# Value products of the prompt's attention in groups of three key blocks, with a compressed branch of fixed width 128, in a decoder step on one core

## The chip, the cores and the metric

The kernel runs on one core of a Trainium2 chip. The metric is the device time of one execution in microseconds, the median of the runs. The engines are named as in the profile: PE is TensorE's matmul, PEld its weight load, DVE is VectorE, ACT is ScalarE, POOL is GpSimd, SP is SyncE.

## What is computed

One layer of a decoder works on 1024 prompt tokens and on 64 sample tokens (8 sequences of 8), with the same weights. Half of its heads are gated linear attention; the other half are sparse attention with 8 query heads on 2 key heads. After them come an output projection, norms and an MLP. The change lies in the sparse attention, which for each query sums three branches, each a softmax of its own, times a gate:

```python
s_c = einsum('bqhgd,bchd->bqhgc', qb, kc) - sl * d_c      # compressed keys: one per 16 tokens
p_c = masked_softmax(s_c, d_c >= 0)
o_c = einsum('bqhgc,bchd->bqhgd', p_c, vc32)
...                                                       # o_s: selected blocks, o_w: window of 512
o_n = gts[..., 0:1] * o_c + gts[..., 1:2] * o_s + gts[..., 2:3] * o_w
```

In the prompt all earlier blocks are selected, so the selected branch there is plain causal attention. The sample tokens attend to a cache of 2048 tokens in pages.

## The kernel before

The instructions are traced by Python code in program order; a planner then sets, at build time, the order on each engine: among the instructions that it holds to be ready, the one that comes first in program order goes first. Each engine runs its own list in that order, and an instruction that isn't ready holds back all that stand behind it on its engine.

**The prompt's attention** (`attention`, lines 1146 to 1250) works in four parts of two query tiles of 128 tokens, in the order `for i in (1, 0, 2, 3)` (line 689). `tt` is the number of the query tile (0 to 7) and `kvh` that of the key head. For each pair of them the loop of lines 1231 to 1247 runs three branches: the compressed one, whose width is `wc = 8 * tt + 8` keys (line 1222), the window (128 to 640 keys) and the selected one (128 to 1024 keys).

- `branch` (line 1163) makes the weights of one branch. For each of four query heads, two matmuls (L1177, L1178) put the scores into a bank of tag `dn`, DVE adds the mask and finds the largest (L1180), ACT takes the exponential (L1184), and POOL scales by gate and sum (L1190). The four results are tiles of tag `Sc`, `Sw` or `Ss`; `SW` and `SS` (line 26) say how many buffers of `Sw` and `Ss` each part has.
- `values` (line 1194) goes over the branch in blocks of 128 keys. For each block PE transposes the four heads' weights into a bank of tag `g`, of which there are three (L1200), ACT copies the bank to a tile `pw`, of which there are three (L1202), and two matmuls add the product with the block's values to the bank `av` (L1205). The first of the two fills partitions 0 to 63 of `av` and the second 64 to 127: each uses 64 of the array's columns. Both are in fp32 and stand as two records each in the trace, so a block has four records at L1205 and four at L1200. The compressed branch is one block, of 8 to 64 rows.

The value products of a branch are traced after the next branch's `branch` (`later`, line 1245), so that scores and softmax of one lie beside the products of the other.

**Fillers.** Other work is traced in between (lines 686 to 696), in proportion to the attention's work as `total` (line 37) counts it: in the first three parts the sample's selection and attention (`sample_select`, `sample_attention`), in the last part the output projection of parts 0 and 1 (`wout`, L259 to L261). The sample's scores (`scores`, line 1343) begin with a matmul that puts mask and distance into the bank (L1345), with 9 or 64 rows of tables in `cstr`, and go on with two matmuls of 64 columns each (L1347). Its own value products (`weigh`, L1384 to L1390) are made in halves of 64 columns, too.

**Order of the work.** The attention begins while the projections before it run out, near 626 us of the trace, and ends near 1062 us, where the output projection of the last two parts and the MLP follow.

Of the kernel before, what the change touches and what calls it, by code (L numbers as in the profile page):

```python
# [9 lines left out]
F32 = mybir.dt.float32  # L10
F32R = mybir.dt.float32r
# [10 lines left out]
BIG = 1e30  # L22
SLOPES = [2.0 ** -(h + 1) for h in range(8)]
CHUNKS = [(0, 384, 384), (384, 384, 384), (768, 256, 320)]
TILES = [(128 * i, 128) for i in range(8)] + [(NP, NS)]
SW, SS = (8, 8, 8, 7), (8, 8, 8, 5)
H2 = [(0, 256), (256, 128), (384, 128), (512, 256), (768, 320)]
# [9 lines left out]
def total(part):  # L37
    return 2 * sum(8 * t + 8 + 128 * min(t + 1, 5) + 128 * (t + 1) for t in (range(6) if part < 3 else (6, 7)))

def shape_constants():
    c = {}
    p = np.arange(128)
    c["ident"] = np.eye(128, dtype=np.float32)
    r = np.arange(-896, 128)
    d = p[:, None] - r[None, :]
    big = {}
    big["m_sel"] = np.where(d >= 0, -d, -BIG).astype(np.float32)
    d = p[:, None] - np.arange(128)[None, :] + 512  # L50
    big["m_old"] = np.where(d <= 512, -d, -BIG).astype(np.float32)
    r = np.arange(-56, 8)
    d = p[:, None] - 16 * r[None, :] - 31
    c["m_cmp"] = np.where(d >= 0, -d, -BIG).astype(np.float32)
    c["row_valid"] = (p >= 31).astype(np.float32)[:, None]
    qs = np.zeros((128, 4), np.float32)
    for j in range(4):
        qs[:64, j] = 0.125 / SLOPES[2 * j]
        qs[64:, j] = 0.125 / SLOPES[2 * j + 1]
    c["qscale"] = qs  # L60
    j, i = p[:, None], p[None, :]
    tri = ((j // 16 == i // 16) & (j <= i)).astype(np.float32) / 16
    bi = (j < 16 * np.arange(10)[None, :]).astype(np.float32) / 16
    c["tri"] = np.concatenate([tri, bi], 1)
    m, q = np.arange(64)[None, :] // 16, p[:, None] // 16
    c["odd"] = (q == 2 * m).astype(np.float32)
    m8 = np.zeros((128, 64), np.float32)
    j, i = np.arange(64)[:, None], np.arange(64)[None, :]
    m8[:64] = (j // 8 == i // 8) & (j <= i)
    c["mask8"] = m8  # L70
    c["tri8"] = m8 / 16
    bm = np.zeros((128, 8), np.float32)
    bm[:] = (np.arange(128) % 64)[:, None] // 8 == np.arange(8)[None, :]
    c["bmask"] = bm
    c["ones"] = np.ones((128, 128), np.float32)
    c["pick"] = (np.isin(p[:, None] - np.arange(24)[None, :], (32, 96))).astype(np.float32)
    return c, big
# [144 lines left out]
class Prog:  # L222
# [845 lines left out]
    def compressed_keys(self, st, st2):  # L1068
        nc, a = self.nc, self.a
        kc = self.pool(st, "kc")  # L1070
        self.KC = self.t(kc, [128, 2, 2, 64], F32R, "KC")
        self.VC = self.t(kc, [64, 2, 64], F32, "VC")
        nc.vector.memset(self.KC.bitcast(F32), 0.0)
# [5 lines left out]
        for kind in range(2):  # L1079
# [7 lines left out]
            ps = self.bank("dn")[:M, :256]  # L1087
# [58 lines left out]
    def attention(self, st):  # L1146
        nc, a = self.nc, self.a
        pool = self.pool(st, "att")
# [10 lines left out]
        nc.vector.tensor_scalar(first, first, self.C("row_valid"), None, op0=OP.mult)  # L1159
        m_sel, m_old, m_cmp = big[:, :1024], big[:, 1024:], self.C("m_cmp")  # L1160


        def branch(tt, kvh, QS, br, vb, k0, pieces):
            K = self.KC[:, kvh] if vb is None else self.KK[vb][:, kvh, :, k0:]
            width = pieces[-1][0] + pieces[-1][1]
            wide = 256 * (tt // 2 + 1)
            shape, tag, bufs = {None: (64, "Sc", 4), 1: (min(640, wide), "Sw", SW[tt // 2]),
                                0: (wide, "Ss", SS[tt // 2])}[vb]
# [24 lines left out]

        def values(av, kvh, S, width, vb, k0, first, last):
            for c in range(0, width, 128):
                cw = min(128, width - c)
                V = self.VC[:cw, kvh] if vb is None else self.VV[:, vb, (k0 + c) // 128, 64 * kvh:64 * kvh + 64]
                pt = self.bank("g")[:cw]
                for g in range(4):
                    nc.tensor.transpose(pt[:, 128 * g:128 * g + 128], S[g][:, c:c + cw], self.C("ident"))  # L1200
                pw = t([128, 512], "pw", 3)[:cw]
                nc.scalar.copy(pw, pt)  # L1202

                for j in range(2):
                    nc.tensor.matmul(av[64 * j:64 * j + 64], V, pw.rearrange("p (a j q) -> p j a q", a=2, j=2)[:, j],  # L1205
                                     start=first and c == 0, stop=last and c + 128 >= width)

        def part_attention(i):
            later = None
            for tt in range(2 * i, 2 * i + 2):  # L1210
# [5 lines left out]
                for j in range(2):  # L1216
# [4 lines left out]
                kend = 128 * (tt + 1)  # L1221
                wc = 8 * tt + 8

                branches = [
                    (0, None, 0, [(0, wc, m_cmp[:, 56 - 8 * tt:64])]),
                    (2, 1, w0, ([(0, 128, m_old)] if tt > 3 else []) +
# [4 lines left out]
                for kvh in range(2):  # L1231
                    box = []
                    for n, (br, vb, k0, pieces) in enumerate(branches):
                        S, width = branch(tt, kvh, QS, br, vb, k0, pieces)

                        def after(box=box, n=n, kvh=kvh, S=S, width=width, vb=vb, k0=k0, catn=self.catn, c0=c0):
                            if n == 0:
                                box.append(self.bank("av")[:, :256].rearrange("p (a q) -> p a q", a=2))
                            values(box[0], kvh, S, width, vb, k0, n == 0, n == 2)
                            if n == 2:  # L1240
                                nc.scalar.copy(catn[:, 2 * kvh:2 * kvh + 2, c0:c0 + 128], box[0])
                            return width


                        if later:
                            yield later()
                        later = after
# [6 lines left out]
    def sample_select(self, keep, pool):  # L1254
# [29 lines left out]
        for pr in range(4):  # L1284
            ps = self.bank("mm")[:, :128]
            self.scores(ps, pr, lambda b2: kc[:, 2 * pr + b2], self.R2("l_t")[:9], self.R2("r_cmp")[:9])
            mx, sm = t([128, 1], "mx", 4), t([128, 1], "sm", 4)
# [72 lines left out]
    def sample_attention(self, pool):  # L1360
# [31 lines left out]

        lt = self.R2("l_t")[:9]
        zero = C("zero")
        for pr in range(4):
            mx, sm = t([128, 3], "mxs", 2), t([128, 2], "sms", 2)
            new = self.R2("oh_tok")[:64, 128 * pr:128 * pr + 128], self.R2("r_new")[:64]
            vc = t([128, 2, 128], "vc")
# [9 lines left out]
            ps = self.bank("mm")  # L1408
            self.scores(ps, pr, lambda b2: wk[:, b2], lt, self.R2("r_win")[:9])
            self.add_max(W[:, :512], ps, zero.to_broadcast([128, 512]), None, mx[:, 0:1])  # L1410
# [17 lines left out]
            for q in range(4):  # L1428
                ps = self.bank("mm")
                self.scores(ps, pr, lambda b2: pages[q][b2][:, :, :128], lt,  # L1430
                            self.R2("r_slc")[:9, None, :].to_broadcast([9, 8, 64]))
                self.add_max(S[:, 512 * q:512 * q + 512].rearrange("p (b i) -> p b i", i=64),
# [336 lines left out]
```

## Time and profile before

| | us |
|---|---|
| median of 3 runs | 1901.11 (1900.35 to 1906.42) |
| the profiled execution, its own time | 1902.94 |
| its span, from first to last instruction | 1901.3 |
| PE busy in the span | 1798.7 (95%) |
| DVE / ACT / POOL busy | 1130.0 / 938.8 / 333.9 |
| mean granted clock of TensorE, as a share of full speed | 0.97 |

The profiled execution is 1.8 us over the median of the runs. Matmul records overlap and their ends are modelled, so PE's busy share doesn't tell how well it is used; the starts of successive records do, and the rows below are read that way: a row's start, subtracted from that of the next row, is what the row took of PE's time.

### The profile page before, as it was taken

Reading aid. Unit: us, or ns where it says so; the run is one execution under the profiler, and the core shown is the slowest. Engines: PE = TensorE matmul, PEld = TensorE weight load, DVE = VectorE, ACT = ScalarE, POOL = GpSimd, SP = SyncE. Lnnn points to the kernel's source line nnn. Section 1 sums busy time; section 2 is a strip of 40 time slices with the busy share of each in tenths; the row PEclk is TensorE's granted clock in tenths of the full one; section 3 lists DMA queues with packets and bytes.
Section 4 is the critical chain, followed back from the end, with each engine's and each line's share of the span. In section 5 each row is a group of like instructions: output and inputs, shape, how many; then the busy total and the mean of one; then the engine's idle time right before and its main releaser. Section 6 shows DMA issues by size and latency. Waiting matters only on the chain.

```text
span 1901.3 us, 33235 instructions
## 1 busy us (share of the span) xinstructions
PE 1798.7 (95%) x12006; PEld 1617.3 (85%) x12006; DVE 1130.0 (59%) x2551; ACT 938.8 (49%) x1913; POOL 333.9 (18%) x502
## 2 busy tenths in 40 slices
PE   4999989999999999999999899999999999999997
PEld 3888889999989755655586799899999999999996
DVE  7867785374434664454636656856566668655555
ACT  4423355353233666555746556543443354654453
POOL 4433210012401446334322100000000001000000
PEclk9999999999999988989999899999999999999998
DMA  7666641113455423213122356321222155564442
GB/s 248 227 228 231 221 138 59 31 47 136 158 192 161 150 75 113 86 56 112 60 70 85 107 194 202 103 78 56 59 75 87 59 157 176 194 205 150 149 151 88
DMA packets 117194, 245.97 MB, mean 129 GB/s; under 512 B 14475, under 2 KB 72637, under 8 KB 116230
## 3 DMA queue, kind: packets, MB, share of 16 engines
q1 hardware_dynamic: 101254, 196.98, 32.6%
q0 software_dynamic: 13328, 43.99, 6.7%
q10 hardware_dynamic: 2448, 2.88, 0.4%
q8 instruction: 94, 1.54, 0.3%
q14 instruction: 70, 0.57, 0.1%
HBM read 215.88 MB, written 32.05 MB: 130 GB/s over the span
## 4 chain that ended last, share of the span: by engine, by line
PE 77%; issue 7%; DVE 7%; DMA 5%; ACT 2%; POOL 1%; SPq 1%; POOLq 0%; DVEq 0%; ACTq 0%
PE mm L259 10%; PE mm L260 10%; PE mm L261 10%; PE dn L259 5%; PE dn L260 5%; PE dn L261 5%; PE g L1200 4%; PE av L1205 4%; PE g L260 3%; PE g L259 3%; PE g L261 3%; PE dn L1177 2%; DMA wr<-w_ada 2%; PE dn L1178 2%; PE mm L1347 1%
## 5 line engine op out<-in xcount | busy, mean ns | idle before, releaser
L254 DVE TENSOR_TENSOR wl<-wr,wh 128x1024 fp32r<-128x1024 f32 x174 | 213.2, 1225 | 215.4 <-ACT wh L253 214.0
L253 ACT CAST wh<-wr 128x1024 fp32r<-128x1024 f32 (+1 forms) x176 | 183.4, 1043 | 241.5 <-PE mm L260 107.8
L259 PE MATMUL dn<-fh,wh 128*128 128x384 f32 (+1 forms) x616 | 204.3, 332 | 5.2 <-DVE fo L1610 2.9
L260 PE MATMUL dn<-fl,wh 128*128 128x384 f32 (+1 forms) x616 | 203.4, 330 | 0.0
L261 PE MATMUL dn<-fh,wl 128*128 128x384 f32 (+1 forms) x616 | 202.9, 330 | 0.0
L599 POOL TENSOR_TENSOR rs_r<-rs_m,mhalf 128x2 f32<-128x2 f32 (+2 forms) x12 | 13.1, 1090 | 710.4 <-DVE rs_m L598 710.4
L259 PE MATMUL mm<-hT,wh 128*128 128x384 f32 (+1 forms) x384 | 128.7, 335 | 6.0 <-ACT st L801 3.4
L260 PE MATMUL mm<-hT,wh 128*128 128x384 f32 (+1 forms) x384 | 128.1, 334 | 0.0
L261 PE MATMUL mm<-hT,wl 128*128 128x384 f32 (+1 forms) x384 | 127.4, 333 | 0.4 <-DVE wl L254 0.4
L259 PEld LDWEIGHTS dn<-fh,wh 128*128 128x128 f32 x616 | 115.7, 188 | 8.1 <-DVE fo L1610 4.2
L260 PEld LDWEIGHTS dn<-fl,wh 128*128 128x128 f32 x616 | 115.8, 188 | 0.3 <-DVE fl L254 0.3
L261 PEld LDWEIGHTS dn<-fh,wl 128*128 128x128 f32 x616 | 115.7, 188 | 0.1
L1202 ACT COPY pw<-g 128x512 f32<-128x512 f32 (+3 forms) x148 | 81.6, 587 | 63.9 <-PE g L1200 63.2
L1610 DVE TENSOR_TENSOR fo<-fo,dn 128x384 f32<-128x384 f32 (+1 forms) x134 | 72.3, 540 | 55.6 <-PE dn L261 55.4
L259 PE MATMUL mm<-w1h,wh 128*128 128x256 f32 x256 | 77.7, 304 | 21.1 <-ACT wh L253 16.2
L1205 PE MATMUL av<-pw,VV 128*64 128x256 f32 x528 | 86.7, 415 | 1.0 <-ACT pw L1202 1.0
L1177 PE MATMUL dn<-KK,QS 128*128 128x512 f32 (+3 forms) x192 | 76.9, 404 | 7.0 <-DVE mx L1180 6.6
L259 PE MATMUL mm<-cth,wh 128*128 128x256 f32 (+1 forms) x256 | 75.9, 298 | 4.5 <-ACT cth L253 4.5
L259 PEld LDWEIGHTS mm<-hT,wh 128*128 128x128 f32 x384 | 73.4, 191 | 7.9 <-ACT st L801 3.6
L261 PE MATMUL mm<-x2h,wl 128*128 128x320 f32 x256 | 79.3, 310 | 0.7 <-DVE wl L254 0.7
L259 PE MATMUL mm<-x2h,wh 128*128 128x320 f32 x256 | 79.2, 309 | 0.0
L260 PE MATMUL mm<-x2l,wh 128*128 128x320 f32 x256 | 79.1, 309 | 0.0
(623 smaller groups left out, 5418.4 us busy)
## 6 DMA issues: line engine op xcount, KB each, us to landing
wr<-w_up SPq DMA_DIRECT2D x72, 512.0 KB, 3.6
wr<-w_down SPq DMA_DIRECT2D x72, 512.0 KB, 3.6
wr<-w_ada SPq DMA_DIRECT2D x48, 512.0 KB, 4.4
wr<-w_f SPq DMA_DIRECT2D x24, 512.0 KB, 3.6
wr<-cw SPq DMA_DIRECT2D x16, 512.0 KB, 4.3
wr<-w_out SPq DMA_DIRECT2D x16, 512.0 KB, 3.5
raw<-cc SPq DMA_DIRECT2D x62, 128.0 KB, 4.8
raw<-cc POOLq DMA_DIRECT2D x61, 128.0 KB, 5.2
```

The lines of the kernel that those rows point to most:

```text
L253: return (self.nc.scalar.copy(h, src), (lo or self.nc.vector).tensor_tensor(l, src, h.bitcast(F32), op=OP.subtract))
L254: (lo or self.nc.vector).tensor_tensor(l, src, h.bitcast(F32), op=OP.subtract))
L259: mm(out, ah, bh, start=start, stop=False)
L260: mm(out, ah, bl, start=False, stop=False)
L261: mm(out, al, bh, start=False, stop=stop)
L1177: nc.tensor.matmul(ps, q, K[:, 0, c:c + cw], start=True, stop=False)
L1178: nc.tensor.matmul(ps, q, K[:, 1, c:c + cw], start=False, stop=True)
L1200: nc.tensor.transpose(pt[:, 128 * g:128 * g + 128], S[g][:, c:c + cw], self.C("ident"))
L1202: nc.scalar.copy(pw, pt)
L1205: nc.tensor.matmul(av[64 * j:64 * j + 64], V, pw.rearrange("p (a j q) -> p j a q", a=2, j=2)[:, j], start=first and c == 0, stop=last and ...
L1347: mm(ps[64 * b2:64 * b2 + 64], self.Q[:, 2 * pr + b2], keys(b2), start=False, stop=True)
L1610: nc.vector.tensor_tensor(o, o, ps, op=OP.add)
```

## The change

In the prompt's attention the value products of a block aren't issued behind the block's copy any more. The block is put on a list, and when three blocks are on it, or the last block of the last branch has come, the products of all are issued one after another. The list runs on over the border from one branch to the next, within one query tile and key head. The products of the first blocks of a group get a dependence on the copy of the last one. There are six `pw` buffers instead of three, and in the last part five and four buffers of `Sw` and `Ss` instead of seven and five.

The compressed branch always works on 128 keys, the later ones masked; its mask, wider now, moves from the table `cst` to `cst3`. `KC`, `VC` and `Sc` grow to 128 keys. The mask matmuls of the sample's scores read all 128 rows of their tables instead of 9 or 64; the added rows are zero on one side.

```diff
+GROUP, PW = 3, 6
-SW, SS = (8, 8, 8, 7), (8, 8, 8, 5)
+SW, SS = (8, 8, 8, 5), (8, 8, 8, 4)
...
-    return 2 * sum(8 * t + 8 + 128 * min(t + 1, 5) + 128 * (t + 1) for t in (range(6) if part < 3 else (6, 7)))
+    return 2 * sum(128 + 128 * min(t + 1, 5) + 128 * (t + 1) for t in (range(6) if part < 3 else (6, 7)))
...
-    r = np.arange(-56, 8)
+    r = np.arange(-56, 128)
     d = p[:, None] - 16 * r[None, :] - 31
-    c["m_cmp"] = np.where(d >= 0, -d, -BIG).astype(np.float32)
+    big["m_cmp"] = np.where(d >= 0, -d, -BIG).astype(np.float32)
...
-        self.KC = self.t(kc, [128, 2, 2, 64], F32R, "KC")
-        self.VC = self.t(kc, [64, 2, 64], F32, "VC")
+        self.KC = self.t(kc, [128, 2, 2, 128], F32R, "KC")
+        self.VC = self.t(kc, [128, 2, 64], F32, "VC")
...
-        def values(av, kvh, S, width, vb, k0, first, last):
+        def values(box, kvh, S, width, vb, k0, last):
             for c in range(0, width, 128):
-                cw = min(128, width - c)
-                V = self.VC[:cw, kvh] if vb is None else self.VV[:, vb, (k0 + c) // 128, 64 * kvh:64 * kvh + 64]
-                pt = self.bank("g")[:cw]
+                V = self.VC[:, kvh] if vb is None else self.VV[:, vb, (k0 + c) // 128, 64 * kvh:64 * kvh + 64]
+                pt = self.bank("g")
                 for g in range(4):
-                    nc.tensor.transpose(pt[:, 128 * g:128 * g + 128], S[g][:, c:c + cw], self.C("ident"))
-                pw = t([128, 512], "pw", 3)[:cw]
-                nc.scalar.copy(pw, pt)
-
-                for j in range(2):
-                    nc.tensor.matmul(av[64 * j:64 * j + 64], V, pw.rearrange("p (a j q) -> p j a q", a=2, j=2)[:, j],
-                                     start=first and c == 0, stop=last and c + 128 >= width)
+                    nc.tensor.transpose(pt[:, 128 * g:128 * g + 128], S[g][:, c:c + 128], self.C("ident"))
+                pw = t([128, 512], "pw", PW)
+                box["group"].append((V, pw, nc.scalar.copy(pw, pt)))
+                end = last and c + 128 >= width
+                if len(box["group"]) < GROUP and not end:
+                    continue
+                for n, (V, pw, ins) in enumerate(box["group"]):
+                    for j in range(2):
+                        m = nc.tensor.matmul(box["av"][64 * j:64 * j + 64], V,
+                                             pw.rearrange("p (a j q) -> p j a q", a=2, j=2)[:, j],
+                                             start=box["first"], stop=end and n == len(box["group"]) - 1)
+                        if n < len(box["group"]) - 1:
+                            tc.add_manual_dep(m.ins, box["group"][-1][2].ins.name, mybir.DependencyInfo(
+                                mybir.DependencyClass.Sync, mybir.DependencyReason.DATA), reason="group")
+                    box["first"] = False
+                box["group"] = []
...
-                    (0, None, 0, [(0, wc, m_cmp[:, 56 - 8 * tt:64])]),
+                    (0, None, 0, [(0, 128, m_cmp[:, 56 - 8 * tt:184 - 8 * tt])]),
...
-        lt = self.R2("l_t")[:9]
+        lt = self.R2("l_t")
...
-            new = self.R2("oh_tok")[:64, 128 * pr:128 * pr + 128], self.R2("r_new")[:64]
+            new = self.R2("oh_tok")[:, 128 * pr:128 * pr + 128], self.R2("r_new")
...
-            self.scores(ps, pr, lambda b2: wk[:, b2], lt, self.R2("r_win")[:9])
+            self.scores(ps, pr, lambda b2: wk[:, b2], lt, self.R2("r_win"))
```

## Rows read from the trace of the kernel before

**Rows 1.** The page: busy us of the engines, their share of the span, instructions.

```profile
PE 1798.7 (95%) x12006; PEld 1617.3 (85%) x12006; DVE 1130.0 (59%) x2551; ACT 938.8 (49%) x1913; POOL 333.9 (18%) x502
```

**Rows 2.** Stretches: length, busy us of PE, PEld, DVE, ACT, POOL; clock, DMA share, GB/s.

```profile
626.00:1062.00 436.00, 415.31 (x2787) 277.30 (x2785) 228.07 (x894) 272.14 (x711) 163.62 (x258) 0.95 0.28 85
...
960.00:1000.00 40.00, 40.00 (x306) 35.12 (x305) 15.48 (x34) 19.05 (x40) 3.44 (x4) 1.00 0.22 67
```

**Rows 3.** Timeline of PE: start, us, instruction, records; a run, and blocks alternating.

```profile
959.64 1.15 PE L1200 MATMUL g<-cst,Ss 128*128 128x128 f32 x9
960.54 0.49 PE L1177 MATMUL dn<-KK,QS 128*128 128x512 f32 x1
...
1055.74 0.66 PE L1200 MATMUL g<-cst,Ss 128*128 128x128 f32 x4
1056.33 0.65 PE L1205 MATMUL av<-pw,VV 128*64 128x256 f32 x4
1056.92 0.66 PE L1200 MATMUL g<-cst,Ss 128*128 128x128 f32 x4
...
1059.84 1.52 PE L1205 MATMUL av<-pw,VV 128*64 128x256 f32 x12
```

**Rows 4.** Timeline of PE: the first row of value products.

```profile
643.17 0.65 PE L1205 MATMUL av<-pw,VC 24*64 24x256 f32 x4
```

**Rows 5.** Timeline of PE: a mask matmul of the sample, and prompt scores before value products.

```profile
701.03 0.31 PE L1200 MATMUL g<-cst,Ss 128*128 128x128 f32 x1
701.27 0.50 PE L1345 MATMUL mm<-cstr 9*128 9x512 f32 x1
701.70 1.08 PE L1347 MATMUL mm<-wr,Q 128*64 128x512 f32 x4
...
1007.46 0.40 PE L1178 MATMUL dn<-KK,QS 128*128 128x512 f32 x1
1007.79 0.65 PE L1205 MATMUL av<-pw,VV 128*64 128x256 f32 x2
```

**Rows 6.** Timeline of PE: scores with 8 and with 128 keys.

```profile
705.43 0.25 PE L1178 MATMUL dn<-KC,QS 128*128 128x8 f32 x1
705.54 0.25 PE L1177 MATMUL dn<-KC,QS 128*128 128x8 f32 x1
...
708.88 0.28 PE L1177 MATMUL dn<-KK,QS 128*128 128x128 f32 x1
708.99 0.27 PE L1178 MATMUL dn<-KK,QS 128*128 128x128 f32 x1
```

**Rows 7.** Lines 1180, 1184, 1190, 1202: count, ns min/median/max, first and last start, forms.

```profile
L1180 DVE CUSTOM_DVE_ANT_0 Sc<-dn,cst x64: 158/192/227, 629.3 to 1015.4; 128x24 f32<-128x24 f32 x8, 128x32 f32<-128x32 f32 x8, 128x8 f32<-128x8 f32 x8, 128x16 f32<-128x16 f32 x8
L1180 DVE CUSTOM_DVE_ANT_0 Sw<-dn,big x64: 277/292/692, 635.0 to 1028.1; 128x128 f32<-128x128 f32 x40, 128x384 f32<-128x384 f32 x8, 128x512 f32<-128x512 f32 x8, 128x256 f32<-128x256 f32 x8
L1184 ACT ACTIVATE Sc<-Sc,mx x64: 284/324/367, 629.5 to 1015.7; 128x24 f32<-128x24 f32 x8, 128x32 f32<-128x32 f32 x8, 128x8 f32<-128x8 f32 x8, 128x16 f32<-128x16 f32 x8
L1184 ACT ACTIVATE Sw<-Sw,mx x64: 384/779/860, 636.0 to 1032.1; 128x640 f32<-128x640 f32 x32, 128x384 f32<-128x384 f32 x8, 128x512 f32<-128x512 f32 x8, 128x128 f32<-128x128 f32 x8
L1190 POOL TENSOR_SCALAR Sc<-Sc,sm,gates x62: 336/367/1352, 639.2 to 1017.8; 128x24 f32<-128x24 f32 x8, 128x32 f32<-128x32 f32 x8, 128x8 f32<-128x8 f32 x8, 128x16 f32<-128x16 f32 x8
L1190 POOL TENSOR_SCALAR Sw<-Sw,sm,gates x62: 437/864/1800, 641.2 to 1036.6; 128x640 f32<-128x640 f32 x30, 128x384 f32<-128x384 f32 x8, 128x512 f32<-128x512 f32 x8, 128x128 f32<-128x128 f32 x8
L1202 ACT COPY pw<-g x148: 558/586/621, 641.6 to 1060.0; 128x512 f32<-128x512 f32 x132, 24x512 f32<-24x512 f32 x2, 32x512 f32<-32x512 f32 x2, 8x512 f32<-8x512 f32 x2
```

**Rows 8.** Who waited for line 1202's copies: us in total, times.

```profile
  PEld av L1205: 6.6, 17
  PE av L1205: 1.0, 3
```

**Rows 9.** Timeline of PE, query tile 6: transposes that free `Sw`, scores into it.

```profile
922.51 0.66 PE L1200 MATMUL g<-cst,Sw 128*128 128x128 f32 x4
...
929.21 0.49 PE L1177 MATMUL dn<-KK,QS 128*128 128x512 f32 x1
```

More of the change, by code (lines that the diff above doesn't have):

```diff
@@ L1146, in attention @@
     def attention(self, st):
-        nc, a = self.nc, self.a
+        nc, tc, a = self.nc, self.tc, self.a
         pool = self.pool(st, "att")
@@ L1159, in attention @@
         nc.vector.tensor_scalar(first, first, self.C("row_valid"), None, op0=OP.mult)
-        m_sel, m_old, m_cmp = big[:, :1024], big[:, 1024:], self.C("m_cmp")
+        m_sel, m_old, m_cmp = big[:, :1024], big[:, 1024:1152], big[:, 1152:]
         def branch(tt, kvh, QS, br, vb, k0, pieces):
@@ L1166, in branch @@
             wide = 256 * (tt // 2 + 1)
-            shape, tag, bufs = {None: (64, "Sc", 4), 1: (min(640, wide), "Sw", SW[tt // 2]),
+            shape, tag, bufs = {None: (128, "Sc", 4), 1: (min(640, wide), "Sw", SW[tt // 2]),
                                 0: (wide, "Ss", SS[tt // 2])}[vb]
@@ L1221, in part_attention @@
                 kend = 128 * (tt + 1)
-                wc = 8 * tt + 8
                 branches = [
-                    (0, None, 0, [(0, wc, m_cmp[:, 56 - 8 * tt:64])]),
+                    (0, None, 0, [(0, 128, m_cmp[:, 56 - 8 * tt:184 - 8 * tt])]),
                     (2, 1, w0, ([(0, 128, m_old)] if tt > 3 else []) +
@@ L1231, in part_attention @@
                 for kvh in range(2):
-                    box = []
+                    box = {"group": [], "first": True}
                     for n, (br, vb, k0, pieces) in enumerate(branches):
@@ L1237, in after @@
                             if n == 0:
-                                box.append(self.bank("av")[:, :256].rearrange("p (a q) -> p a q", a=2))
-                            values(box[0], kvh, S, width, vb, k0, n == 0, n == 2)
+                                box["av"] = self.bank("av")[:, :256].rearrange("p (a q) -> p a q", a=2)
+                            values(box, kvh, S, width, vb, k0, n == 2)
                             if n == 2:
-                                nc.scalar.copy(catn[:, 2 * kvh:2 * kvh + 2, c0:c0 + 128], box[0])
+                                nc.scalar.copy(catn[:, 2 * kvh:2 * kvh + 2, c0:c0 + 128], box["av"])
                             return width
@@ L1285, in sample_select @@
             ps = self.bank("mm")[:, :128]
-            self.scores(ps, pr, lambda b2: kc[:, 2 * pr + b2], self.R2("l_t")[:9], self.R2("r_cmp")[:9])
+            self.scores(ps, pr, lambda b2: kc[:, 2 * pr + b2], self.R2("l_t"), self.R2("r_cmp"))
             mx, sm = t([128, 1], "mx", 4), t([128, 1], "sm", 4)
@@ L1430, in sample_attention @@
                 self.scores(ps, pr, lambda b2: pages[q][b2][:, :, :128], lt,
-                            self.R2("r_slc")[:9, None, :].to_broadcast([9, 8, 64]))
+                            self.R2("r_slc")[:, None, :].to_broadcast([128, 8, 64]))
                 self.add_max(S[:, 512 * q:512 * q + 512].rearrange("p (b i) -> p b i", i=64),
```

## The prediction, put down before the change was run

> **What bounds the kernel now.** I read four views, in this order. The page puts PE at 95% of the span, far over DVE and ACT [rows 1], so what shortens PE's list shortens the kernel, if PE is really at work in the stretch that changes. The table by stretches shows that for the attention, 626 to 1062 us: PE 415 of 436 us, DVE 228, ACT 272, POOL 164 [rows 2]. So PE is the bound there, with some 21 us of visible idle time. The granted clock tells a second thing: its mean is 0.95, against 1.00 at 960 to 1000 us, where the output projection fills PE [rows 2]. As the levels are 2.4 and 1.2 GHz, 0.95 means a tenth of the stretch, some 44 us, at the lower one, which costs at most half of that, 22 us.
>
> The third view, PE's timeline, shows what those 415 us hide. The starts tell what a row takes. Nine transposes in a row take 960.54 - 959.64 = 0.90 us, or 0.10 each. Where single blocks alternate, the four transposes of one take 1056.33 - 1055.74 = 0.59 us, against 0.40 to 0.44 for the same four in a row, and the products of one 1056.92 - 1056.33 = 0.59 us. Three blocks' products in a row are a row of 1.52 us against 0.65 for one, so a further block costs (1.52 - 0.65) / 2 = 0.43 [rows 3]. Each way between full-width matmuls and products of 64 columns thus loses about 0.15 us (0.59 - 0.44, and 0.59 - 0.43): **0.30 us for a visit to the products and back**, however many blocks it holds. No engine is waited for in these rows; the array itself changes over.
>
> The fourth view, the count. There are 148 blocks (the copies in the row of line 1202 [rows 7]). From the first row of products [rows 4] to the last [rows 3] the timeline has some 125 runs of them, nearly all of four records, one block. 125 visits at 0.30 are 38 us of the stretch.
>
> **The change, part by part.**
>
> *Fewer visits.* A query tile and key head has 1 + min(tt + 1, 5) + tt + 1 blocks: 3, 5, 7, 9, 11, 12, 13, 14 for tt = 0 to 7. In threes, with the rest, these are 1, 2, 3, 3, 4, 4, 5, 5 groups, over two heads 54. All products of a group become ready with one copy, so they come out in one run unless something that stands before them in program order becomes ready in between. I take 60 runs, ends 54 and 90. Of the 125 runs now, about a tenth stand right beside other products in halves (the sample's), where a visit has less to lose. So (125 - 60) x 0.30 x 0.93 = 18 us less; ends (125 - 90) x 0.30 x 0.93 = 10 and (125 - 54) x 0.30 = 21.
>
> *The sample's mask matmul.* With 9 rows it takes 701.70 - 701.27 = 0.43 us before the products in halves follow, and 0.24 lie between the transpose before it and itself, against 0.10 between transposes. A matmul over 128 rows of as many columns is followed by products in halves after 1007.79 - 1007.46 = 0.33 us [rows 5]. So full rows save some 0.10 behind it and 0.10 ahead. There are 32; 20 have 512 columns, 12 fewer, for which I count the 0.10 ahead alone: 20 x 0.20 + 12 x 0.10 = 5.2 us, less the ten or so that come right behind products in halves and have nothing to save ahead: 4 us. Ends 2 and 6.
>
> *128 keys in the compressed branch.* On PE, 128 score matmuls grow from 8 to 64 columns to 128. From one to the next it is 0.11 us with 8 columns and 0.11 with 128 [rows 6], as another weight load lies between, so I count 0. The Trainium skill says otherwise (TensorE: Matmul & The Clock Gate, Back-to-back issue gap): some 60 cycles up to 64 columns, 134 at 128. By it each would take 74 cycles more, an estimate of 31 ns at 2.4 GHz, 4 us in all, and the sum below would be 16 us. The trace doesn't agree with it for these pairs. Elsewhere the branch pays: DVE's mask step takes 0.19 us (median) for `Sc` and 0.28 to 0.29 for 128 keys (the window's least and median), ACT's exponential 0.32 against 0.38 (the window's least, 128 keys) [rows 7]; 64 of each, 6.4 and 3.8 us. POOL's step I bound by ACT's, the same number of elements: under 4 us. All three engines have 160 us or more free in the stretch [rows 2], and these scores are made a branch ahead of their transposes. 0; without that cover the chain of four heads would show, 0.5 us in each of 16 rounds: 8 us.
>
> *The new wait.* A group's first product stands on PE's list behind its third copy. What stands behind it there is everything else of PE: the next blocks' transposes, scores, fillers, and through them DVE's mask steps and ACT's copies. Today products wait 6.6 + 1.0 us for copies, 20 times [rows 8], since each is listed with other PE work before it. A copy takes 0.59 us [rows 7], a block's transposes 0.44, so the third copy of a group ends about 3 x 0.59 - 3 x 0.44 + 0.44 = 0.9 us after the third block's transposes, if ACT does nothing else. There are three `g` banks, so the next block's transposes (0.44) can go in that gap as soon as the first copy has freed one, beside scores and fillers. I take 2 us more of waiting in all; ends -5 (54 waits in place of 148) and 8 (half of the groups, 0.3 each).
>
> *Buffers and fillers.* In the last part `Sw` falls to five, `Ss` to four. Five mean that of the second key head's four `Sw` tiles one is free at once. Before, its last scores stood at 929.21 anyway, 6.7 us after the last transposes of the first head's tiles began at 922.51 [rows 9]; the heads two and three can start no later than that last one does. 0, upper end 4. The new `total` moves a few fillers by one step: 0. A wider `cst3` is one load long before its use: 0.
>
> *The sum.* -18 - 4 + 0 + 2 + 0 = **-20 us**, all of it on PE's list in the attention, against the profiled execution's 1902.9 (its span and 1.6 us around it): 1883. That execution is 1.8 us over the median of the runs, so on the median it is 1881, and I say **1880**. What is late next is still PE: the stretch would be 416 us with DVE at 234 and ACT at 276.
>
> **The rivals.**
>
> *The clock rises, too (about 1869).* If the time at 1.2 GHz comes from changing over, 65 visits fewer take part of it away. For: 960 to 1000 us, with hardly a change-over, has 1.00 [rows 2]. Half of the 22 us back is -11: 1880 - 11.
>
> *The groups don't hold (about 1892).* If the planner puts other work between the products of a group, or lists them so late that PE idles, the change does little of what it says: a third of the visits' gain, 6, and the 4 of the mask matmuls, less 2: 8 to 10 us, 1892. Against: of the runs now nearly none is shorter than a block, though a block is four records that could be parted as well.
>
> *The clock falls (about 1900, no change).* Twelve transposes now come in a row, then a gap for the copy. If the array counts as idle during them, the lower level takes 88 us instead of 44 and gives back 22. Against: nine transposes in a row stand just before a stretch at 1.00 [rows 2, 3]. The Trainium skill states the rule behind it (TensorE: Matmul & The Clock Gate, PE-mode transpose: they don't count as busy); these rows neither need nor exclude it.
>
> *Slower (about 1911): the third copy.* PE's list is rigid. If ACT, with exponentials and weight splits on the same list, gets to the third copy late, PE stands still before every group. One whole copy of 0.59 us [rows 7] in each of 54 groups is 32 us, against the 22 that visits and mask matmuls give: +10. It decides from 22 / 54 = 0.41 us a group. For: ACT is busy 272 of 436 us [rows 2], and one of its exponentials takes up to 0.86 [rows 7]. Against: 148 such waits cost 7.6 us today, 0.05 each [rows 8].
>
> **How the numbers follow.** A measurement of this kernel can tell about 0.3% (5.7 us) from no change: faster is below 1895.4, slower above 1906.8. Chances: the forecast 0.63, clock rises 0.12, groups don't hold 0.10, clock falls 0.08, third copy 0.07. The forecast's own ends: 10 to 21 for the visits, 2 to 6 for the mask matmuls, -5 to 8 for the wait; taken together, as they won't all fall to one side, 1871 to 1890. The range reaches over that to the rising clock and to the groups that don't hold, each with a little around it: 1866 to 1893. It leaves out a third of the first rival (0.04) and the last two (0.15). Faster: 0.63 + 0.12 + most of 0.10 = 0.84; same: the rest of that and the falling clock, 0.09; slower 0.07.
>
> **What would show it.** Right: rows of products with twelve records in place of four and 54 to 65 runs; 0.43 us for each further block; 0.11 us between the compressed branch's scores at 128 columns; a mask matmul that products in halves follow after 0.33; the attention about 416 us long, and the time before and behind it unchanged. Wrong: more than 15 us of waits for line 1202's copies, a mean clock in the attention under 0.93, or more than 90 runs.

## The result, and the profile after

| kernel | median us | range | ratio to before, 95% interval |
|---|---|---|---|
| before | 1900.73 | 1899.79 to 1906.42 (4 runs) | |
| changed | 1883.74 | 1876.84 to 1884.36 (4 runs) | 0.9884 [0.9857, 0.9911] |

The changed kernel is 17 us faster; 1880 was predicted, with a range of 1866 to 1893. Its profiled execution took 1883.71 us, with a span of 1882.0.

The page after: busy time, share and instructions of the engines, to be read beside [rows 1].

```profile
PE 1773.6 (94%) x12006; PEld 1621.5 (86%) x12006; DVE 1137.7 (60%) x2551; ACT 943.2 (50%) x1913; POOL 340.7 (18%) x502
```

The table by stretches of the changed kernel: the attention with a little beside it, as in [rows 2], and 960 to 1000 us. Columns as there.

```profile
627.00:1045.00 418.00, 391.17 (x2808) 285.34 (x2806) 237.03 (x895) 275.87 (x711) 168.43 (x257) 0.97 0.30 91
960.00:1000.00 40.00, 40.00 (x316) 36.36 (x313) 17.72 (x43) 22.45 (x45) 4.41 (x4) 1.00 0.21 62
```

Against [rows 2], PE is busy 24 us less (415 to 391). The same number of matmuls is issued in the whole kernel, 12006. So the gain is inside PE's busy time, not in its gaps: visible idle time went from 21 to 27 us. A part of these 24 us, some 10, goes with the clock, as the table below shows. ACT is busy 276 us, as predicted, DVE 237 (234 was said). The mean clock went from 0.95 to 0.97.

PE's timeline after shows the groups: a compressed block and two others, a whole group of twelve records, the last run.

```profile
995.10 0.49 PE L1202 MATMUL g<-cst,Sw 128*128 128x128 f32 x3
995.52 0.65 PE L1210 MATMUL av<-pw,VC 128*64 128x256 f32 x4
996.00 1.03 PE L1210 MATMUL av<-pw,VV 128*64 128x256 f32 x8
996.97 0.51 PE L1178 MATMUL dn<-KK,QS 128*128 128x512 f32 x1
...
1001.26 1.52 PE L1210 MATMUL av<-pw,VV 128*64 128x256 f32 x12
1002.71 0.33 PE L1178 MATMUL dn<-KC,QS 128*128 128x128 f32 x1
...
1041.11 1.53 PE L1202 MATMUL g<-cst,Ss 128*128 128x128 f32 x12
1042.56 2.72 PE L1210 MATMUL av<-pw,VV 128*64 128x256 f32 x20
```

From 1001.26 to 1002.71 three blocks take 1.45 us, 0.48 each, change-over included; alternating single blocks took 0.59 each [rows 3]. The rows at 995.52 and 996.00 are one run, as only the name of the second operand differs. Counted so, products come in 52 runs, 40 of them of twelve records, where 131 runs stood before (113 of four records).

The table of waits for the weight loads (PEld), attention alone, changed kernel: who waited for what, us in total, times, longest. "Issue" means that nothing the profile shows was waited for.

```profile
PEld g L1202 <- issue: 10.5, 30, 0.4
PEld dn L1178 <- issue: 10.1, 19, 0.8
...
PEld av L1210 <- issue: 4.0, 18, 0.4
...
PEld mm L1355 <- issue: 2.6, 7, 0.8
```

The same view of the kernel before has, for these four:

```profile
PEld g L1200 <- issue: 32.1, 81, 0.8
...
PEld dn L1177 <- issue: 12.4, 23, 1.6
PEld av L1205 <- issue: 11.6, 53, 0.4
...
PEld mm L1345 <- issue: 4.6, 17, 0.8
```

This is the change-over, seen from the other side: a weight load of 128 columns that follows products of 64 columns, or the reverse, comes late, and no other engine is named. Of all such waits of the loads in the attention, 223 of 232 stand before, and 123 of 130 after, where the rows or columns in use change from one matmul to the next. At transposes and products together there were 134 before and 48 after. The sum of all such rows in the attention went from 75 to 41 us. (Loads run beside matmuls, so these 34 us are not all PE's path.) The Trainium skill says as much without a price (TensorEngine Tiling (Array Packing), Key Properties: a change of the tiling mode, not of the tile alone, drains the array); these rows agree with it, and [rows 3] give the price.

To compare kernels I took PE's attention apart, from the first score to the last product, by the starts of its records. Each interval to the next start is the row's own pace (0.109 us for a transpose, columns / 2.4 GHz + 0.012 for a full matmul, 0.21 for a pair of products in halves), plus 0.148 us for each change, from one matmul to the next, of the part of the array in use (all 128 rows or fewer, and the number of columns; a transpose counts as 128 columns), plus what is left. The price is half of the 0.30 of [rows 3]; there are 397 such changes before and 232 after. What is left is put under "low clock" where 1.2 GHz was granted, else under "waits". Change-overs are thus a count times a price; "waits" is a remainder, and another rule for the intervals at the edges of the low clock moves some 3 us between the two.

```
us                             attention  pace  change-overs  waits  low clock  runs  after it
before                           433.4   317.7     58.8       35.2     21.4      131    839.8
changed                          412.8   318.1     34.3       48.1     11.8       52    836.6
changed, two further profiles    418.6   317.3     34.3       44.3     22.3       52    837.5
                                 410.4   317.3     34.3       48.7      9.7       52    839.2
groups of one                    422.7   317.5     52.9       39.7     12.6      126    846.6
groups of two                    406.4   318.9     38.9       39.0      9.1       75    843.9
groups of four                   405.3   319.4     32.6       42.5     10.4       46    841.7
mask rows as before              417.2             37.6       45.3     16.7       52    837.9
full mask rows alone             424.9             55.2       37.4     13.7      131    839.0
compressed blocks narrow again   422.1   317.7     36.6       46.0     21.4       53    841.1
second copy on DVE               417.2             34.3       50.6     13.4       55    838.1
```

From before to changed: change-overs -24.5, waits +13, low clock -10, in sum -20.6 us of the attention. Without its "low clock" the attention is 412.0 us before, 396 to 401 in the changed kernel's three profiles and 410.1 with groups of one. The time before the attention was 4.6 us longer in this profile and that behind it 3.2 shorter. Neither is the change's: over all profiles, of whichever kernel, the attention began between 622.7 and 637.3 us.

### The profile page after: what moved, and what is told of

Read it like the earlier page. It is cut to its first block, busy times and chain, and to the rows that moved or that the text cites. A ratio compares the mean times of both kernels' runs of the same rounds, so it can differ in the third digit from the quotient of the medians.

```text
span 1882.0 us, 33223 instructions
## 1 busy us (share of the span) xinstructions
PE 1773.6 (94%) x12006; PEld 1621.5 (86%) x12006; DVE 1137.7 (60%) x2551; ACT 943.2 (50%) x1913; POOL 340.7 (18%) x502
## 4 chain that ended last, share of the span: by engine, by line
PE 77%; DMA 8%; DVE 7%; ACT 3%; issue 2%; SPq 1%; POOL 1%; DVEq 0%; POOLq 0%; ACTq 0%
PE mm L260 11%; PE mm L261 11%; PE mm L262 11%; PE dn L260 5%; PE dn L261 5%; PE dn L262 5%; PE g L1202 3%; PE av L1210 3%; PE g L262 3%; PE g L260 3%; PE g L261 3%; DMA xt<-xT 2%; PE dn L1178 2%; DMA wr<-w_ada 2%; PE dn L1179 2%
## 5 line engine op out<-in xcount | busy, mean ns | idle before, releaser
L1204 ACT COPY pw<-g 128x512 f32<-128x512 f32 x148 | 81.3, 590 | 37.0 <-PE g L1202 36.4
L262 PE MATMUL mm<-w1h,wl 128*128 128x256 f32 x256 | 76.2, 298 | 1.5 <-DVE wl L255 1.5
```

The source lines that it names most:

```text
L262: mm(out, al, bh, start=False, stop=stop)
L1204: box["group"].append((V, pw, nc.scalar.copy(pw, pt)))
```

## The experiments

Two theories: the gain is the fewer visits (grouping), or it comes from the parts beside it, the full mask rows and the wider compressed branch. And two further questions: what the waits are that grew by 13 us, and whether three is the right size.

**Groups of one**, all else as in the changed kernel:

```diff
-GROUP, PW = 3, 6
+GROUP, PW = 1, 6
```

> The changed kernel with groups of one block: every other part of the change stays (128 compressed keys, full rows in the sample's mask matmuls, six pw buffers, fewer Sw and Ss). Theory A (change-overs of the array): the visits to the value products go from 52 runs back to about 130, so some 23 us of the gain go, 0.30 us each, less the low clock that comes and goes with it; time 1897 to 1906, about 130 runs of four records, change-overs worth about 55 us in the attention. Theory B (the gain came from the clock and from the other parts, the groups only move waits): time within 5 us of the changed kernel, 1879 to 1889.

Measured 1899.61 us (10 runs, 1893.14 to 1905.01), ratio 0.9968 [0.9949, 0.9987]. Runs of products go back to 126. The loads' waits show what came back:

```profile
PEld g L1202 <- issue: 30.9, 76, 0.8
...
PEld av L1210 <- issue: 12.6, 57, 0.4
```

Those are the numbers of the kernel before (32.1 and 11.6). Without grouping a third of a per cent is left of the gain; grouping makes the rest, 9 to 16 us by the changed kernel's three ratios (0.9884 here, 0.9911 and 0.992 below). The clock isn't what parts the two: over all runs its mean is 0.9745 with groups of one and 0.972 to 0.976 in the changed kernel. By the profiles 4 to 12 us of the difference lie in the attention (change-overs 18.6 us more, waits 5 to 9 less) and 7 to 10 behind it, where no cause was looked for.

**Full mask rows alone**, on the kernel before (five places, two of them here). PE's instructions stand in the same order as before:

```diff
-        lt = self.R2("l_t")[:9]
+        lt = self.R2("l_t")
...
-            self.scores(ps, pr, lambda b2: wk[:, b2], lt, self.R2("r_win")[:9])
+            self.scores(ps, pr, lambda b2: wk[:, b2], lt, self.R2("r_win"))
```

> The kernel before with full rows in the sample's mask matmuls and nothing else; PE's order the same as before. Theory A: 4 us faster than before, 1895 to 1899, with 0.33 us instead of 0.43 behind a mask matmul of 512 columns. Theory B (PE's saved time turns into waits for other engines or pages): less than 1 us faster.

Measured 1895.62 us (10 runs), ratio 0.996 [0.9937, 0.9984]: -7.6 us, with 3 to 12 in the interval. The timeline of this kernel, a mask matmul (L1345) between a transpose and products in halves, to be read beside [rows 5]:

```profile
704.88 0.31 PE L1200 MATMUL g<-cst,Ss 128*128 128x128 f32 x1
704.94 0.49 PE L1345 MATMUL mm<-cstr 128*128 128x512 f32 x1
705.36 1.08 PE L1347 MATMUL mm<-wr,Q 128*64 128x512 f32 x4
```

Ahead of it 0.06 us (median 0.03 where a transpose stands ahead), against 0.24 in [rows 5] (median 0.20): saved. Behind it 0.42, against 0.43: not saved. By the starts the 14 mask matmuls that follow a transpose save some 0.17 us ahead and 0.02 behind. Six of the seven that follow a prompt score of 512 columns save 0.09 ahead and 0.10 behind, so there the 0.33 of [rows 5] does come (0.32 and 0.33 at 836 and 839 us of this run's trace). Those that follow products in halves save nothing. Together that is about 3 us. The other 4 us of the median are not in the change-overs; in its profile the stretch at 1.2 GHz cost 13.7 us in place of 21.4.

**Mask rows as before**, in the changed kernel: the same five places, the other way round.

> The changed kernel with the sample's mask matmuls on 9 and 64 rows again, PE's order the same as in the changed kernel. Theory A (row count changes the array over, too): 0.43 us between such a matmul with 512 columns and the products in halves behind it, 0.2 between the transpose before it and itself, 4 us slower in all (2 to 6): about 1888. Theory B (the rows' number is free, as the other engines' waits hide it): within 1 us of the changed kernel.

Measured 1887.03 us (4 runs), ratio 0.989 [0.9859, 0.9921]. PE's order is that of the changed kernel, change-overs grow by 3.3 us in the trace. The time can't tell it from the changed kernel's own 0.9884 to 0.992. So the mask matmuls are worth about 3 us; a direct difference in time is not shown.

**Fewer `Sw` and `Ss` alone**, on the kernel before:

```diff
-SW, SS = (8, 8, 8, 7), (8, 8, 8, 5)
+SW, SS = (8, 8, 8, 5), (8, 8, 8, 4)
```

> The kernel before with five Sw and four Ss buffers in the last part instead of seven and five, nothing else. The prediction counted 0 for this (upper end 4 us): the kernel before within 1 us, 1900 to 1902. The rival: the second key head's scores wait for the first one's transposes and some of the 13 us of waits that the changed kernel has more than before come from there: 3 to 8 us slower, in the last part of the attention.

Measured 1901.63 us (10 runs), ratio 0.9978 [0.9958, 0.9999]; the attention took 433.3 us, 433.4 before. It costs nothing, as counted. That its interval lies just under 1 shows that 0.2% between two medians isn't yet an effect here; the 0.3 and 0.4% of groups of one and of full mask rows alone are little more.

**The changed kernel again**, twice, as a yardstick for the kernels run beside it:

> The changed kernel again, to stand beside groups of two, four and six on one chip, and to tell which differences of its trace repeat. From the first scores to the end of the attention 413 us (410 to 417), 52 runs of products, and 45 to 50 us of PE's time in the attention that is neither work at its usual pace nor change-over nor low clock (35 before). Its ratio to the kernel before 0.986 to 0.992.

> The changed kernel beside the next three on one chip, in five rounds, since differences of 2 to 5 us are asked. Ratio to the kernel before 0.987 to 0.991; attention 413 to 419 us from the first scores to the last product.

Measured 1887.05 us (6 runs), 0.9911 [0.9884, 0.9938], and 1887.28 (6 runs, 1880.8 to 1892.77), 0.992 [0.9896, 0.9945]. Over the three sets of runs the gain is 15 to 22 us by the ratios; the last ratio and its attention of 410.4 us lie just outside what was expected. Of the same program, one profile has an attention of 418.6 us at a mean clock of 0.94, the other 410.4 at 0.98; these are their rows in the table by stretches, each of its own attention:

```profile
634.00:1053.00 419.00, 392.49 (x2763) 283.92 (x2762) 232.00 (x889) 274.73 (x712) 168.93 (x257) 0.94 0.28 87
```

```profile
629.00:1040.00 411.00, 384.39 (x2778) 279.01 (x2777) 233.25 (x892) 272.70 (x707) 168.24 (x256) 0.98 0.29 90
```

So how long 1.2 GHz is granted changes from one execution to the next by 27 us in the attention, with the same work in the same order. Of a single profile, up to 12 us are this.

**Other sizes of group**: `GROUP` 2, 4 and 6, and 4 again.

> Groups of two blocks, everything else as changed; 75 runs of products in PE's list instead of 52. Theory A (0.30 us a visit, waits as they are): 23 visits more, 7 us slower than the changed kernel in the same call (5 to 9). Theory B (a group waits for its last copy, and smaller groups wait less): waits fall by some 4 us, so 1 to 4 us slower.

> Groups of four blocks with the same six pw buffers; 46 runs of products instead of 52. Theory A: 6 visits fewer, 2 us faster than the changed kernel, or the same within a microsecond. Theory B (the group holds its pw buffers and PE waits for the last copy; with four of six buffers held, the next group's copies have two): 3 to 8 us slower, with waits of products for copies over 12 us where the changed kernel has 10.

> Groups of six blocks with six pw buffers, so that a group holds them all; 34 runs of products instead of 52. Theory A: 18 visits fewer, 5 us faster than the changed kernel. Theory B: no copy of the next group can begin before the first products of this one are through, and with three g banks the transposes stop too: PE's waits grow by more than the 5 us, 3 to 15 us slower than the changed kernel.

> Groups of four again, in five rounds beside groups of three: does a larger group gain anything? By visits alone (46 runs against 52) 2 us faster than the changed kernel. If what PE saves is taken back as waits at the start of the MLP, as the runs with two, four and six blocks showed (some 6 us between the 300th and the 500th matmul behind the attention): the same within 3 us, with the attention 6 to 10 us shorter and the rest 6 us longer.

| group | median us | ratio | change-overs, us | runs |
|---|---|---|---|---|
| 1 | 1899.61 | 0.9968 [0.9949, 0.9987] | 52.9 | 126 |
| 2 | 1885.16 | 0.9915 [0.9894, 0.9936] | 38.9 | 75 |
| 3 | 1883.74 to 1887.28 | 0.9884 to 0.992 | 34.3 | 52 |
| 4 | 1881.86, 1880.52 | 0.9891 [0.9868, 0.9915], 0.9885 [0.9856, 0.9914] | 32.6 | 46 |
| 6 | 1882.09 | 0.9896 [0.9872, 0.9919] | 28.9 | 34 |

The step from one to two is nearly all of it. From two on the intervals overlap. Neither two blocks in a group, for which both theories expected it, nor four or six, for which theory B did, were slower than three. Four was below three both times they ran side by side, by 5 and 7 us of the median; it may be the better one, but the intervals don't part them. The attention gets shorter with the size, 405.3 us with four and 402.0 with six, and the time behind it longer, 841.7 and 842.8.

Groups of two have an attention 6 us shorter than the changed kernel's, but the time behind it is 7 us longer (843.9 against 836.6; 837.5 and 839.2 in the changed kernel's further profiles), and so the whole is the same. The table by stretches shows it for the same 36 us behind the attention, first of groups of two, then of the changed kernel:

```profile
1090.00:1126.00 36.00, 32.65 (x194) 30.59 (x193) 22.66 (x44) 20.46 (x41) 3.03 (x4) 1.00 0.78 249
```

```profile
1099.00:1135.00 36.00, 35.55 (x220) 35.23 (x220) 25.99 (x47) 24.41 (x46) 2.75 (x4) 1.00 0.70 224
```

PE, which was full there, stands idle for 3 us, and the timeline of groups of two names what it waits for, the first operand of the next stage and weights:

```profile
1107.39 0.62 PE L260 MATMUL mm<-x0h,wh 128*128 128x384 f32 x2 [1.31 <-ACT x0h L254]
...
1111.00 0.44 PE L260 MATMUL mm<-x0h,wh 128*128 128x384 f32 x1 [1.00 <-ACT c L1591]
...
1112.21 0.44 PE L262 MATMUL mm<-x0h,wl 128*128 128x384 f32 x1 [0.59 <-DVE wl L255]
```

It is a hint of the next bound: ACT, DVE and the loads (249 GB/s) are late there when PE comes earlier. The cause was not tested.

**Compressed blocks narrow again** (8 tt + 8 keys in place of 128 masked ones), in groups of three:

```diff
-            shape, tag, bufs = {None: (128, "Sc", 4), 1: (min(640, wide), "Sw", SW[tt // 2]),
+            shape, tag, bufs = {None: (64, "Sc", 4), 1: (min(640, wide), "Sw", SW[tt // 2]),
...
-                V = self.VC[:, kvh] if vb is None else self.VV[:, vb, (k0 + c) // 128, 64 * kvh:64 * kvh + 64]
-                pt = self.bank("g")
+                cw = min(128, width - c)
+                V = self.VC[:cw, kvh] if vb is None else self.VV[:, vb, (k0 + c) // 128, 64 * kvh:64 * kvh + 64]
+                pt = self.bank("g")[:cw]
...
-                    nc.tensor.transpose(pt[:, 128 * g:128 * g + 128], S[g][:, c:c + 128], self.C("ident"))
-                pw = t([128, 512], "pw", PW)
+                    nc.tensor.transpose(pt[:, 128 * g:128 * g + 128], S[g][:, c:c + cw], self.C("ident"))
+                pw = t([128, 512], "pw", PW)[:cw]
...
-                    (0, None, 0, [(0, 128, m_cmp[:, 56 - 8 * tt:184 - 8 * tt])]),
+                    (0, None, 0, [(0, 8 * tt + 8, m_cmp[:, 56 - 8 * tt:64])]),
```

> The changed kernel with the compressed branch 8 to 64 keys wide again, its block still in a group with two blocks of 128 keys; 53 runs of products in PE's list. Theory A (fewer rows in the products are another arrangement of the array, so the narrow block costs a change-over inside its group, 16 times 0.15 to 0.30 us): 2 to 5 us slower than the changed kernel, with more than the 209 ns between the last narrow product and the first one of 128 rows. Theory B (padding costs DVE, ACT and POOL 14 us in all, some of which shows): 1 to 5 us faster.

Measured 1898.15 us (12 runs, 1892.46 to 1909.59), ratio 0.9975 [0.9957, 0.9993]: 11 us slower than the changed kernel run beside it, which neither theory had expected. The timeline shows the mechanism that was looked for:

```profile
655.70 0.65 PE L1211 MATMUL av<-pw,VC 24*64 24x256 f32 x4
656.28 1.08 PE L1211 MATMUL av<-pw,VV 128*64 128x256 f32 x8
```

From the compressed block to the next it is 0.58 us, against 0.48 in the changed kernel (995.52 to 996.00 above): a change from 24 rows to 128 interrupts a run although the columns stay 64. But that is 16 places, some 2.4 us with both sides counted. The rest of the 11 is not accounted for: in its profile the clock's mean was 0.94 and "low clock" 10 to 12 us above two of the changed kernel's three profiles, but not above the third; over all runs the mean clock was 0.969 against 0.972 beside it, which is 0.3% of the span at most, 6 us. Without "low clock" its attention takes 400.7 us, no more than the changed kernel's 396 to 401. So the time shows that the kernel with narrow blocks is slower; its profile doesn't show that the cut runs make it so, and what does stays open.

**The second copy of a group on DVE**, to test whether ACT's copies are the new waits:

```diff
-                box["group"].append((V, pw, nc.scalar.copy(pw, pt)))
+                cp = nc.vector.tensor_copy if len(box["group"]) == 1 else nc.scalar.copy
+                box["group"].append((V, pw, cp(pw, pt)))
```

> The changed kernel with the copy of every group's second block on DVE, so that the third copy stands behind one other copy of its group on ACT, not two. Theory A (the 8 to 13 us of added waits in the attention come from the wait for the third copy): waits of products for copies fall from 9.8 us to under 5, and the time by 3 to 6 us. Theory B (those waits are small and the rest of the added waits comes from scores, masks and scaling that a shorter list of PE no longer covers): waits of the products fall a little, the time stays within 2 us or gets longer, as DVE's copies stand among the mask steps.

Measured 1892.56 us (6 runs), ratio 0.9943 [0.992, 0.9965]: 5 us slower by the median than the changed kernel run beside it, though the intervals overlap. PE's waits in the attention, first with that copy on DVE, then of the changed kernel:

```profile
PE dn L1178 <- DVE mx L1181: 14.7, 27, 1.2
...
PE av L1211 <- ACT pw L1205: 1.3, 3, 0.6
```

```profile
PE dn L1178 <- DVE mx L1181: 5.9, 16, 1.0
PE g L1202 <- POOL Sw L1191: 4.7, 8, 1.5
...
PE av L1210 <- ACT pw L1204: 2.8, 3, 1.3
PE g L1202 <- ACT pw L1204: 1.3, 3, 0.5
```

Half of PE's waits for copies went away (1.5 us), and 9 us came in at the scores, whose bank DVE frees with the mask step. So theory B held: less waiting for copies did not shorten the kernel where DVE has to make some of them.

## Why the prediction was right, point by point

*What bounds the kernel.* Right: 24 us came out of PE's busy time in the attention (some 10 of them by the clock), none out of its gaps. A share of 95% that hides change-overs was the point, and the starts, not the durations, showed it [rows 3].

*Fewer visits, -18 (10 to 21).* Right in mechanism and count: 131 runs to 52, where 125 to 60 was predicted. The fall of change-overs is 24.5 us with the mask matmuls, 21 without; by the runs, 79 x 0.30 x 0.93 = 22. The term was 3 to 4 us too small, since the groups hold even better than taken. Groups of one give 18.6 us of change-overs back, and 9 to 16 us of time.

*The mask matmul, -4 (2 to 6).* The sum held, about 3 us, but one step in it failed: the 0.10 behind it. The 0.33 us of [rows 5] was measured behind prompt scores that value products follow; behind most mask matmuls of 512 columns it stays 0.40 to 0.43 with 9 rows or with 128. Only where a prompt score of 512 columns stands ahead is the 0.10 saved. Ahead, 0.17 was saved behind a transpose and not 0.10. The nearest row was not near enough: what stands ahead of the pair counts too.

*128 keys, 0.* Right in sum. From one compressed score to the next it is 0.11 us at 128 columns in places such as this:

```profile
636.93 0.28 PE L1179 MATMUL dn<-KC,QS 128*128 128x128 f32 x1
637.04 0.27 PE L1178 MATMUL dn<-KC,QS 128*128 128x128 f32 x1
637.15 0.28 PE L1179 MATMUL dn<-KC,QS 128*128 128x128 f32 x1
```

But the two rows of [rows 6] compare a head's second score to the next with 8 keys and a first to a second with 128, and these steps differ. From a head's first score to its second it is 0.14 us with 128 keys (median of 59 outside the low clock) against 0.11 before (58), and from the second on 0.11 in both. Where transposes follow, the first of them gives this back, with 0.13 us in place of 0.16: from the last but one transpose ahead to the third behind it is 0.63 to 0.64 us in both kernels (four places before, five after). The Trainium skill's table (TensorE: Matmul & The Clock Gate, Back-to-back issue gap), by which I had estimated 4, thus fits the difference at one step in two, and not the sum of these pairs of weight load and matmul. The dearer steps of DVE, ACT and POOL stayed covered, as far as the time shows. What the prediction missed is that the wider block is of use: with a narrow one the kernel is 11 us slower.

*The new wait, +2 (-5 to 8).* This is the term that was mis-sized. Where it was looked for it was about right: products waited for copies 7.6 us before [rows 8] and 9.8 after (7.0 + 2.8). A step was left out: the transposes behind them wait for the `g` banks that the copies free, 4.7 us, which no row shows before. These are the lines of the changed kernel's copies, who waited for them:

```profile
  PEld av L1210: 7.0, 14
...
  PEld g L1202: 3.4, 5
  PE av L1210: 2.8, 3
...
  PE g L1202: 1.3, 3
```

Together 14.5 against 7.6: 7 us in place of 2, though the loads' part of it runs in part beside matmuls. In PE's own rows of waits (19.2 us before, 25.4 after, close to the visible idle time of 21 and 27) copies make only half of the growth, 1.0 to 4.1. As much comes from a wait that the prediction didn't name: transposes wait for POOL's scaling, first before, then after:

```profile
PE g L1200 <- POOL Ss L1190: 3.5, 1, 3.5
PE g L1200 <- POOL Sw L1190: 2.7, 6, 1.0
```

```profile
PE g L1202 <- POOL Sw L1191: 4.7, 8, 1.5
...
PE g L1202 <- POOL Ss L1191: 3.7, 6, 2.3
...
PE g L1202 <- POOL Sc L1191: 0.9, 1, 0.9
```

That is 6.2 against 9.3 us; what makes POOL late there was not tested. The remainder that I called waits grew by 13, by 9 to 14 in the three profiles; for what goes beyond these rows no cause is shown. Two or four blocks in a group have 39 and 42 us, so it isn't grouping as such. It also isn't the third copy that the slower rival named: 0.41 us a group was needed for that, and 7 us over 54 groups are 0.13.

*The clock, 0.* "Low clock" fell from 21.4 to 11.8 us in the first profile, so the rival in which the clock rises looked right for a part. Two further profiles of the same kernel have 22.3 and 9.7. Over all runs the granted clock's mean went from 0.968 to 0.969 up to 0.972 to 0.976. In the 51 runs of the kernel before that stand beside the experiments, 0.001 more of mean clock goes with 1.4 us less; by that the two later sets of runs of the changed kernel, 0.004 and 0.005 over the kernel beside them, have an estimated 5 and 7 us from the clock. It isn't the change-overs that the clock goes with, as the rival had it: groups of one have 357 changes and a clock of 0.9745, and groups of three with narrow compressed blocks 247 changes and 0.969. What it does go with is the compressed branch: over the runs of each kernel the mean is 0.9707 to 0.9760 with 128 keys and 0.9676 to 0.9705 with fewer. No run tells why. So the clock gave something where the prediction had 0. In the first profile it about makes up for the waits, and that is why the total came out near the forecast: two terms were off, by 10 each, and against each other. That is luck; the terms of visits and mask matmuls are not. The clock did not fall: with twelve transposes in a row its mean in the attention was 0.94 to 0.98, which is not below the 0.95 of before by more than it changes from run to run.

*Buffers and fillers, 0.* Right, by the run with fewer buffers alone.

*The sum.* -18 - 4 + 2 = -20 was predicted; -24.5 + 13 - 9.6 + 0.4 was found in the profile, -20.6 of attention, and -17 in the medians.

## What to carry to other kernels

Read the cost of a matmul from the distance between starts, not from its duration, and do it for each order in which the kinds follow each other; here a PE that was 95% busy spent 14% of its attention on change-overs (58.8 of 433.4 us). Collect the matmuls that leave part of the array unused into runs; here the first doubling of the run brought most of it, and what longer runs took off the attention came back in part behind it. Try the odd block as high as the others, even with masked keys: here that was worth 11 us, of which the cut runs explain some 2.4.

## What was not expected of the hardware

A change of the rows alone, with 64 columns on both sides, costs too: from products over 24 keys to products over 128 keys 0.58 us in place of 0.48. Behind most mask matmuls of 512 columns it is 0.40 to 0.43 us to the next product in halves whether they have 9 rows or 128, and 0.33 behind prompt scores of 512 columns [rows 5]; with 128 rows and such a score ahead it is 0.32 to 0.33 there, too. No run tells why. And the same program in the same order was granted 1.2 GHz for 20 us of its attention in one execution and for 48 in another, on another chip.
